# Start and end of a two-layer decoder trunk: whole first weight tiles, x cast in one piece, more idle products, another order of the last down products

## The chip, the core and the metric

The kernel runs on one core of a Trainium2 chip. The time is the device time of one execution in microseconds; lower is better. Only the matrix engine (TensorE, PE in the rows) multiplies; ScalarE (ACT) and VectorE (DVE) prepare its operands, GpSimd (POOL) does little, and SyncE (SP) issues the transfers from main memory.

## The reference

Two layers, each a half-step SwiGLU feed-forward block (FFN), a token mixer, and a second FFN. The sequence is 256 tokens of width 1024, the FFN is 2816 wide. All is float32.

```python
def swiglu(x, w_gate, w_up, w_down):
    return (jax.nn.silu(x @ w_gate) * (x @ w_up)) @ w_down

for l in range(DEPTH):
    x = layer_norm(ALPHA * x + 0.5 * swiglu(x, ffn1_gate[l], ffn1_up[l], ffn1_down[l]), ln_g[l, 0], ln_b[l, 0])
    ...
    x = layer_norm(ALPHA * x + mix, ln_g[l, 1], ln_b[l, 1])
    x = layer_norm(ALPHA * x + 0.5 * swiglu(x, ffn2_gate[l], ffn2_up[l], ffn2_down[l]), ln_g[l, 2], ln_b[l, 2])
```

## The kernel before

**Products in three parts.** Every float32 operand is split into a high half (a cast to the type fp32r, by ScalarE) and a low half (the operand minus the high half, by VectorE); `halves` does both (lines 102 and 103). `mm3` then makes one product out of three (lines 96 to 98), in this order: x high by weight high, x high by weight low, x low by weight high. The second one is therefore the first that needs the weight's low half.

**Weights.** They come in tiles of 128 x 1024 floats (512 KB) through five raw buffers: a transfer on SyncE (line 140), then `halves` into a ring of finished tiles. A tile of gate and up weights holds two of the eight steps of the width 1024, here kt 0 to 7: kt 0 and 1 in weight 0, kt 2 and 3 in weight 1, and so on; the left 512 columns belong to the even kt. The width of the FFN is cut into 11 groups (`NG`), of 256 gate and 256 up columns; the tokens into two halves (`hf`) of 128.

**The start.** The first group's four weights are not loaded as all the others are. `FFN.start` (the first FFN only) cuts each of them into two halves of 512 columns, and x, which lies transposed in memory, into pieces of 1, 1, 2, 2 and 2 kt (`cuts`). SyncE issues a piece of x and then the weight halves that go with it. The order of ScalarE and VectorE is written out by hand in a string: `X2` splits the third piece of x (for each token half apart), `W3` the half of a weight for kt 3, `M3` issues the six products of kt 3 (`pair`: three for either token half). TensorE's own order is by hand everywhere: the order of the code. While the first transfers are on their way, TensorE does `WARM` products of a tile of zeros (line 381).

**The rest.** Behind the start a scheduler orders ScalarE and VectorE, with priorities for the steps that TensorE waits for; the order of TensorE and the transfers' order stay that of the code.

**The end.** `D(g, hf)` multiplies group g's result by its two down weights: six products into the left accumulator (`c` = 0, columns 0 to 511), then six into the right one (`c` = 1). The last calls are D(8, 1), D(9, 1) and D(10, 1); behind the last one `layer_norm` (lines 252 to 262) adds the residual and takes statistics of either half on VectorE, and the result is stored. The operand of D(10, 1) is transposed by TensorE (line 409) and split by ScalarE and VectorE only while D(9, 1) runs: a counter of products (`later`) puts the transposes behind the fourth of the `mm3` calls that follow.

Of the kernel before, what the change touches and what calls it, by code (L numbers as in the profile page):

```python
# [10 lines left out]
F32 = mybir.dt.float32  # L11
# [3 lines left out]
ALU = mybir.AluOpType  # L15
PSUM = bass.MemoryType.PSUM

P = 128
D = 1024
# [5 lines left out]
NG = DFF // GW  # L25
# [13 lines left out]
AHEAD, BEHIND = 100, 400  # L39
PINNED, STARTED = 4, 4  # L40
HT = 6
WARM = 14


class Later:
# [29 lines left out]
def trunk(ctx: ExitStack, tc: tile.TileContext, t, out: bass.AP):  # L75
    nc = tc.nc
# [30 lines left out]
    class Weight:  # L107


        def __init__(self, src, ring, bufs, cuts=1):  # L110
            self.src, self.ring, self.bufs, self.cuts = src, ring, bufs, cuts
            self.uses = 2
            self.parts = None
            stream.append(self)

        def load(self):
            p = wp if self.ring == "w" else scope[0]
            older = rings.setdefault(self.ring, []) if p else None
            if p is None or len(older) >= self.bufs and older[-self.bufs].uses:
                return False  # L120
            older.append(self)
            self.raw = rawp.tile([P, ET], F32, name="raw")
            wh = p.tile([P, ET], F32R, name=self.ring + "h", bufs=self.bufs)
            wl = p.tile([P, ET], F32R, name=self.ring + "l", bufs=self.bufs)
            self.parts = (wh, wl)
            if self.cuts == 1:
                self.fetch(0)
                first, second = self.split(0)
                if position[0] < STARTED + 6:
                    tc.keep_in_program_order(first)  # L130
                if pinned[0]:
                    tc.keep_in_program_order(second)
                pinned[0] = max(0, pinned[0] - 1)
            return True
# [134 lines left out]
    class FFN:  # L269
        def __init__(self, l, w, ln_i, first=False, last=False):  # L270
            gu, dn = t["gu"][l, w], t["dn"][l, w]
            self.first, self.last, self.mixer_next = first, last, not w
            self.slots = ((16, 18), (16, 18) if w else (13, 14))
            self.accs = [None, None]
            self.gw, self.dw, self.ht = {}, {}, {}
            self.ln = (l, ln_i)
            self.gb = None
            for g in range(NG):
                self.gw[g] = []
                for kq in range(4):  # L280
                    extra = (4 * g + kq) % (NW + NX) >= NW
                    self.gw[g].append(Weight(gu[g, kq], *(("x", NX) if extra else ("w", NW)),
                                             2 if first and g == 0 else 1))
                for n in {0: [], 1: [0, 1], 2: [], NG - 1: [NG - 2, NG - 1]}.get(g, [g - 1]):
                    self.dw[n] = [Weight(dn[2 * n + i], "d", ND) for i in range(2)]

# [62 lines left out]
        def start(self):  # L349

            ws = self.gw[0]
            for w in ws:
                w.load()
            position[0] = STARTED
            pinned[0] = 6
            cuts = (0, 1, 2, 4, 6, 8)
            xr = [xp.tile([P, KT // 2, S], F32, name="x") for _ in range(2)]
            arrived = lambda a, b: xr[a // 4][:, a % 4:a % 4 + b - a, :]
            for a, b in zip(cuts, cuts[1:]):
                nc.sync.dma_start(arrived(a, b), t["xT"][:, a:b, :])  # L360
                for k in range(a, b):
                    ws[k // 2].fetch(k % 2)
            for hf in range(2):
                xT[hf] = Transposed(hf, None, cuts=cuts)
            ps = [psa.tile([P, 2 * GW], F32, name="acc") for _ in range(2)]

            def split_x(n):
                a, b = cuts[n], cuts[n + 1]
                for hf in range(2):
                    halves(xT[hf].h[:, a:b, :], xT[hf].l[:, a:b, :], arrived(a, b)[:, :, hf * P:(hf + 1) * P])  # L370
                    xT[hf].done = b

            def multiply(kt):
                self.pair(kt, ws, ps)


            zero = scope[0].tile([P, 256], mybir.dt.bfloat16, name="zero")
            nc.vector.memset(zero, 0.0)
            idle = psg.tile([P, 512], F32, name="gu")[:, 0:256]
            for _ in range(WARM):  # L380
                nc.tensor.matmul(idle, zero[:, 0:P], zero, start=True, stop=True)
            with tc.manual_schedule(engines={mybir.EngineType.Activation, mybir.EngineType.DVE}):
                for what in "X0 W0 M0 X1 W1 M1 X2 W2 M2 W3 M3 X3 W4 M4 W5 M5 X4 W6 M6 W7 M7".split():
                    {"X": split_x, "W": lambda k: ws[k // 2].split(k % 2), "M": multiply}[what[0]](int(what[1]))
            for w in ws:
                w.uses = 0
            advance()
            for hf in range(2):
                self.gate(0, hf, ps[hf])
            ps = [psg.tile([P, 2 * GW], F32, name="gu") for _ in range(2)]  # L390
            for kt in range(KT):
                self.pair(kt, self.gw[1], ps)
                if kt % 2:
                    self.gw[1][kt // 2].uses = 0
                    advance()
            for hf in range(2):
                self.gate(1, hf, ps[hf])
# [15 lines left out]
                halves(hth, htl, pt)  # L413
            self.ht[g, hf] = (hth, htl)

        def D(self, g, hf):
            if self.turned(g):
                ht = [[p[:, place[hf], :] for p in self.ht[g, i]] for i in range(2)]
            else:
                later.wait(lambda: (g, hf) in self.ht)  # L420
                ht = [[p[:, i, :] for p in self.ht[g, hf]] for i in range(2)]
            if g == 0:
                self.accs[hf] = [psa.tile([P, 512], F32, name="acc") for _ in range(2)]
            if g == 4 and hf == 0:
                self.gb = load_gb(*self.ln)
                if self.first:
                    load_consts()
                    for n in range(2):
                        load_x(n)
            dw = [w.parts for w in self.dw[g]]  # L430
            for c in range(2):
                cs = slice(c * 512, c * 512 + 512)
                for i in range(2):
                    mm3(self.accs[hf][c], ht[i][0], ht[i][1], dw[i][0][:, cs], dw[i][1][:, cs],
                        g == 0 and i == 0, g == NG - 1 and i == 1)
            for w in self.dw[g]:
                w.used()
            if g == NG - 1:
                layer_norm(hf, self.accs[hf], 0.5 / ALPHA, self.gb, self.slots[hf], self.last)

        def run(self):
# [29 lines left out]
            if self.first:  # L471
                with tc.high_priority(offset=-BEHIND):
                    lower_bounds()
            for g in range(NG - 3, NG):
                D(g, 1)


    def lower_bounds():
# [399 lines left out]
```

## Time and profile before

| | us |
|---|---|
| three runs | 966.07, 968.62, 968.62 |
| median | 968.62 |
| the profiled execution, its time | 968.72 |
| its span, first to last instruction | 967.0 |
| TensorE busy | 956.0 |
| VectorE busy | 653.5 |
| ScalarE busy | 520.0 |

The span and all rows are of one profiled execution. A time of the trace counts from the first instruction. In a row of the timeline the first number is the start, the second the length; a row that ends in x2 holds two instructions, and brackets give the engine's idle time ahead of it and what ended that. A product's length in these rows is longer than its step, since products overlap: how fast TensorE goes is read from the distance of two starts.

### The profile page before, as it was taken

The page shows a single profiled execution, that of the slowest core. Times are in us where ns is not written, and L with a number is a line of the kernel's source. Part 1 is how long each engine was busy: PE and PEld are TensorE (multiplying, and loading weights), DVE is VectorE, ACT ScalarE, POOL GpSimd, SP SyncE. Part 2 cuts the span into 40 slices and gives each one's busy share as a digit, 9 for nine tenths or more (in the row PEclk, how much of TensorE's full clock was granted, in tenths as well). Part 3 has the DMA queues.
Part 4 walks back from the last instruction along what each step waited for, and adds up shares of the span by engine and source line. Part 5 has one row for each costly group of instructions (what it writes and reads, how often), then busy time and mean ns, then how long its engine had stood idle before and what let it go on. Part 6 is the DMA issues. An engine that isn't in the chain of part 4 may idle for free. (4 is left out here: it accounts for less than half of the span.)

```text
span 967.0 us, 13131 instructions
## 1 busy us (share of the span) xinstructions
PE 956.0 (99%) x4814; PEld 806.9 (83%) x4814; DVE 653.5 (68%) x1093; ACT 520.0 (54%) x808; POOL 27.7 (3%) x50
## 2 busy tenths in 40 slices
PE   9999999999999999999999999999999999999996
PEld 7888888888887888888888888888888888888885
DVE  6875656669679775756676565647897896665625
ACT  6766554367455656454446555433965466645420
POOL 0000000010010000000000000000001000000000
PEclk9999999999999999999999999999999999999999
DMA  8977775333436867564346766543334377766301
GB/s 282 339 257 264 253 244 175 112 109 132 154 109 215 308 218 240 191 208 168 119 162 242 236 209 215 167 153 98 129 133 155 103 266 282 228 224 205 127 1 44
DMA packets 51521, 180.68 MB, mean 187 GB/s; under 512 B 6272, under 2 KB 6528, under 8 KB 51456
## 3 DMA queue, kind: packets, MB, share of 16 engines
q1 hardware_dynamic: 51264, 179.31, 55.2%
q8 instruction: 38, 0.62, 0.2%
q0 software_dynamic: 192, 0.53, 0.2%
q14 instruction: 27, 0.22, 0.1%
HBM read 178.76 MB, written 1.05 MB: 186 GB/s over the span
## 5 line engine op out<-in xcount | busy, mean ns | idle before, releaser
L102 ACT CAST wh<-raw 128x1024 fp32r<-128x1024 f32 (+1 forms) x204 | 210.1, 1034 | 110.2 <-DMA raw<-in_gu 40.7
L103 DVE TENSOR_TENSOR wl<-raw,wh 128x1024 fp32r<-128x1024 f32 (+1 forms) x204 | 241.4, 1198 | 24.8 <-ACT wh L102 12.7
L310 PE MATMUL gu<-xt,wh 128*128 128x512 f32 x768 | 180.6, 391 | 0.0
L103 DVE TENSOR_TENSOR dl<-raw,dh 128x1024 fp32r<-128x1024 f32 x88 | 106.9, 1223 | 100.2 <-ACT dh L102 99.9
L310 PEld LDWEIGHTS gu<-xt,wh 128*128 128x128 f32 x768 | 144.1, 188 | 31.5
L102 ACT CAST dh<-raw 128x1024 fp32r<-128x1024 f32 x88 | 92.0, 1050 | 108.3 <-DMA raw<-in_dn 104.0
L96 PE MATMUL acc<-dh,hth 128*128 128x512 f32 x352 | 139.9, 397 | 0.0
L98 PE MATMUL acc<-dh,htl 128*128 128x512 f32 x352 | 138.2, 393 | 0.0
L97 PE MATMUL acc<-dl,hth 128*128 128x512 f32 x352 | 137.5, 391 | 0.2 <-DVE dl L103 0.2
L96 PE MATMUL gu<-wh,xt 128*128 128x512 f32 x336 | 135.0, 402 | 0.0
L98 PE MATMUL gu<-wh,xt 128*128 128x512 f32 x336 | 131.6, 392 | 0.0
L97 PE MATMUL gu<-wl,xt 128*128 128x512 f32 x336 | 131.3, 391 | 0.0
L310 PE MATMUL gu<-xt,wl 128*128 128x256 f32 x768 | 99.6, 282 | 0.0
L310 PEld LDWEIGHTS gu<-xt,wl 128*128 128x128 f32 x768 | 96.8, 191 | 1.9
L333 DVE TENSOR_TENSOR sil<-gu,sil 128x256 f32<-128x256 f32 x64 | 27.0, 422 | 92.0 <-ACT sil L332 92.0
L98 PEld LDWEIGHTS acc<-dh,htl 128*128 128x128 f32 x352 | 66.0, 188 | 14.8
L97 PEld LDWEIGHTS acc<-dl,hth 128*128 128x128 f32 x352 | 66.2, 188 | 13.2 <-DVE dl L103 0.8
L96 PEld LDWEIGHTS acc<-dh,hth 128*128 128x128 f32 x352 | 66.2, 188 | 12.0
L98 PEld LDWEIGHTS gu<-wh,xt 128*128 128x128 f32 x336 | 63.1, 188 | 13.6
L97 PEld LDWEIGHTS gu<-wl,xt 128*128 128x128 f32 x336 | 63.2, 188 | 12.6
L96 PEld LDWEIGHTS gu<-wh,xt 128*128 128x128 f32 x336 | 63.1, 188 | 12.4
L310 PE MATMUL gu<-xt,xh 128*128 128x512 f32 x256 | 62.4, 396 | 0.0
(157 smaller groups left out, 1026.7 us busy)
## 6 DMA issues: line engine op xcount, KB each, us to landing
raw<-in_gu SPq DMA_DIRECT2D x172, 512.0 KB, 4.3
raw<-in_dn SPq DMA_DIRECT2D x88, 512.0 KB, 4.6
raw<-in_win SPq DMA_DIRECT2D x40, 512.0 KB, 4.4
raw<-in_wout SPq DMA_DIRECT2D x16, 512.0 KB, 4.3
lng<-in_ln_g SPq DMA_DIRECT2D x6, 512.0 KB, 4.5
lnb<-in_ln_b SPq DMA_DIRECT2D x6, 512.0 KB, 5.8
raw<-in_gu SPq DMA_DIRECT2D x8, 256.0 KB, 6.3
raw<-in_cumM SPq DMA_DIRECT2D x2, 512.0 KB, 5.1
```

Of the source, the lines that this page charges most:

```text
L96: nc.tensor.matmul(ps, lh, wh, start=start, stop=False)
L97: nc.tensor.matmul(ps, lh, wl, start=False, stop=False)
L98: nc.tensor.matmul(ps, ll, wh, start=False, stop=stop)
L102: first = nc.scalar.copy(dst_h, src)
L103: return first, nc.vector.tensor_tensor(dst_l, src, dst_h.bitcast(F32), ALU.subtract)
L310: nc.tensor.matmul(ps[i][part][:, 2 * S - w:], weight.parts[lo][:, c:c + P], x[:, 0:w], start=kt == 0 and not lo, stop=kt == KT - 1 and lo ...
L333: nc.vector.tensor_tensor(dst, p[:, 0:S], dst, ALU.add)
```

## The change

- The first group's weights: only weight 0 is still fetched and split in two halves. Weights 1, 2 and 3 are fetched by one transfer of 512 KB each and split by one cast of 1024 columns and one subtraction. The new parameter `by_hand` keeps all four out of the usual loading.
- Of each pair of transfers the weight's is now issued first, then the piece of x. Since there are as many pieces of x as fetches (five), the whole weight 1 now goes ahead of the x piece of kt 2 and 3, weight 2 ahead of that of kt 4 and 5.
- A piece of x is split for both token halves by one instruction; the first piece's cast is done by VectorE, not ScalarE.
- `WARM` is 17 instead of 14.
- In the last FFN the last three D of the second token half are taken by halves of columns, in the order (8, left), (9, left), (8, right), (10, left), (9, right), (10, right).

```diff
-WARM = 14
+WARM = 17
...
-            if self.cuts == 1:
+            if not self.by_hand:
                 self.fetch(0)
...
-                                             2 if first and g == 0 else 1))
+                                             2 if first and g + kq == 0 else 1, first and g == 0))
...
             for a, b in zip(cuts, cuts[1:]):
+                ws[a // 2].fetch(a % 2)
                 nc.sync.dma_start(arrived(a, b), t["xT"][:, a:b, :])
-                for k in range(a, b):
-                    ws[k // 2].fetch(k % 2)
...
                 a, b = cuts[n], cuts[n + 1]
+                h, l = (xt2[:, a:b, m].rearrange("p k h t -> p k (h t)") for m in range(2))
+
+                (nc.vector.tensor_copy if n == 0 else nc.scalar.copy)(h, arrived(a, b))
+                nc.vector.tensor_tensor(l, arrived(a, b), h.bitcast(F32), ALU.subtract)
                 for hf in range(2):
-                    halves(xT[hf].h[:, a:b, :], xT[hf].l[:, a:b, :], arrived(a, b)[:, :, hf * P:(hf + 1) * P])
                     xT[hf].done = b
...
-                for what in "X0 W0 M0 X1 W1 M1 X2 W2 M2 W3 M3 X3 W4 M4 W5 M5 X4 W6 M6 W7 M7".split():
+                for what in "X0 W0 M0 X1 W1 M1 X2 W2 M2 M3 X3 W4 M4 M5 X4 W6 M6 M7".split():
...
-        def D(self, g, hf):
+        def D(self, g, hf, cols=(0, 1)):
...
-            for c in range(2):
+            for c in cols:
...
+            if 1 not in cols:
+                return
...
-            for g in range(NG - 3, NG):
-                D(g, 1)
+            if self.last:
+
+                for g, c in ((NG - 3, 0), (NG - 2, 0), (NG - 3, 1), (NG - 1, 0), (NG - 2, 1), (NG - 1, 1)):
+                    D(g, 1, (c,))
+            else:
+                for g in range(NG - 3, NG):
+                    D(g, 1)
```

The order of SyncE's first transfers, before (raw is the buffer of a weight, in_gu the gate and up weights, x a piece of x):

```order
L360 DMA x<-in_xT 128x256
L140 DMA raw<-in_gu 128x512
L360 DMA x<-in_xT 128x256
L140 DMA raw<-in_gu 128x512
L360 DMA x<-in_xT 128x512
L140 DMA raw<-in_gu 128x512 x2
L360 DMA x<-in_xT 128x512
L140 DMA raw<-in_gu 128x512 x2
```

and now:

```order
L140 DMA raw<-in_gu 128x512
L361 DMA x<-in_xT 128x256
L140 DMA raw<-in_gu 128x512
L361 DMA x<-in_xT 128x256
L140 DMA raw<-in_gu 128x1024
L361 DMA x<-in_xT 128x512
L140 DMA raw<-in_gu 128x1024
L361 DMA x<-in_xT 128x512
```

The third piece of x (the first of 128x512) stood behind two half weights and two pieces; now two half weights, two pieces and the whole weight 1 stand ahead of it.

VectorE at the start, before (xt is the split x, wl the low half of a weight, zero the tile of zeros):

```order
L378 MEMSET zero 128x128
L103 TENSOR_TENSOR xt<-x,xt 128x128 x2
L103 TENSOR_TENSOR wl<-raw,wh 128x512
L103 TENSOR_TENSOR xt<-x,xt 128x128 x2
L103 TENSOR_TENSOR wl<-raw,wh 128x512
L103 TENSOR_TENSOR xt<-x,xt 128x2x128 x2
L103 TENSOR_TENSOR wl<-raw,wh 128x512 x2
```

and now:

```order
L380 MEMSET zero 128x128
L370 CAST xt<-x 128x256
L371 TENSOR_TENSOR xt<-x,xt 128x256
L103 TENSOR_TENSOR wl<-raw,wh 128x512
L371 TENSOR_TENSOR xt<-x,xt 128x256
L103 TENSOR_TENSOR wl<-raw,wh 128x512
L371 TENSOR_TENSOR xt<-x,xt 128x2x256
L103 TENSOR_TENSOR wl<-raw,wh 128x1024
```

The first piece's cast came to VectorE, and the low half for kt 2 is one of 1024 columns; ScalarE's list has the same pieces in the same turn, its cast of weight 1 being one of 128x1024.

TensorE before its last products, before (one row of each six; acc_7611 is the left accumulator, acc_7612 the right one; hth_8583, hth_8735 and hth_8906 are of groups 8, 9 and 10):

```order
L96 MATMUL acc_7611<-dh_8462,hth_8583 128x512
...
L96 MATMUL acc_7612<-dh_8462,hth_8583 128x512
...
L96 MATMUL acc_7611<-dh_8614,hth_8735 128x512
...
L96 MATMUL acc_7612<-dh_8614,hth_8735 128x512
...
L96 MATMUL acc_7611<-dh_8670,hth_8906 128x512
...
L96 MATMUL acc_7612<-dh_8670,hth_8906 128x512
```

and now (acc_7595 is the left one, acc_7596 the right one; hth_8567, hth_8719 and hth_8890 are of groups 8, 9 and 10):

```order
L96 MATMUL acc_7595<-dh_8446,hth_8567 128x512
...
L96 MATMUL acc_7595<-dh_8598,hth_8719 128x512
...
L96 MATMUL acc_7596<-dh_8446,hth_8567 128x512
...
L96 MATMUL acc_7595<-dh_8654,hth_8890 128x512
...
L96 MATMUL acc_7596<-dh_8598,hth_8719 128x512
...
L96 MATMUL acc_7596<-dh_8654,hth_8890 128x512
```

The left half of group 10 moved from the fifth place to the fourth; the transposes of line 409 stand behind the second six in both.

## Rows read from the trace of the kernel before

**Rows 1.** Page, part 1: each engine's busy time, share of span, instructions.

```profile
PE 956.0 (99%) x4814; PEld 806.9 (83%) x4814; DVE 653.5 (68%) x1093; ACT 520.0 (54%) x808; POOL 27.7 (3%) x50
```

**Rows 2.** TensorE's waits: line, for whom, us in total, times, longest.

```profile
PE acc L96 <- ACT wh L102: 0.9, 1, 0.9
PE gu L186 <- DVE x L260: 0.7, 1, 0.7
```

**Rows 3.** Timeline, TensorE, the first 19 us.

```profile
1.06 3.17 PE L381 MATMUL gu<-zero 128*128 128x256 bf16 x14 [1.06 <-DVE zero L378]
5.15 0.79 PE L96 MATMUL acc<-wh,xt 128*128 128x512 f32 x1 [0.92 <-ACT wh L102]
5.88 0.79 PE L97 MATMUL acc<-wl,xt 128*128 128x512 f32 x1
...
9.45 0.63 PE L96 MATMUL acc<-wh,xt 128*128 128x512 f32 x1
9.88 0.55 PE L97 MATMUL acc<-wl,xt 128*128 128x512 f32 x1
10.26 0.39 PE L98 MATMUL acc<-wh,xt 128*128 128x512 f32 x1
10.49 0.39 PE L96 MATMUL acc<-wh,xt 128*128 128x512 f32 x1
10.71 0.47 PE L97 MATMUL acc<-wl,xt 128*128 128x512 f32 x1
...
18.76 0.39 PE L96 MATMUL gu<-wh,xt 128*128 128x512 f32 x1
```

**Rows 4.** Timeline, ScalarE, the first 17 us.

```profile
4.48 0.62 ACT L102 CAST wh<-raw 128x512 fp32r<-128x512 f32 x1 [0.79 <-DMA raw<-in_gu]
...
8.38 0.71 ACT L102 CAST xt<-x 128x256 fp32r<-128x256 f32 x2 [1.87 <-DMA x<-in_xT]
9.29 1.28 ACT L102 CAST wh<-raw 128x512 fp32r<-128x512 f32 x2 [0.21 <-DMA raw<-in_gu]
...
15.29 1.05 ACT L102 CAST wh<-raw 128x1024 fp32r<-128x1024 f32 x1 [0.65 <-DMA raw<-in_gu]
```

**Rows 5.** Timeline, VectorE, the first 18 us.

```profile
9.94 1.36 DVE L103 TENSOR_TENSOR wl<-raw,wh 128x512 fp32r<-128x512 f32 x2 [0.36 <-ACT wh L102]
...
16.37 1.23 DVE L103 TENSOR_TENSOR wl<-raw,wh 128x1024 fp32r<-128x1024 f32 x1 [1.00 <-ACT wh L102]
```

**Rows 6.** Timeline, SyncE: issues of x's third piece and weight 1.

```profile
2.59 0.44 SPq L360 DMA_DIRECT2D x<-in_xT  x1
3.07 0.91 SPq L140 DMA_DIRECT2D raw<-in_gu  x2
```

**Rows 7.** Transfers issued at 2.7:3.0 and 3.6:3.9; last number, us from issue to landing.

```profile
x<-in_xT SPq DMA_DIRECT2D x1, 256.0 KB, 5.8
...
raw<-in_gu SPq DMA_DIRECT2D x1, 256.0 KB, 6.4
```

**Rows 8.** Stretches: length, busy time of each engine, granted clock, DMA share, GB/s.

```profile
3.00:6.00 3.00, 2.08 (x8) 0.97 (x6) 1.37 (x5) 1.62 (x6) 0.00 (x0) 1.00 0.82 253
6.00:9.00 3.00, 3.00 (x7) 2.35 (x8) 1.10 (x4) 1.13 (x3) 0.00 (x0) 1.00 0.92 246
9.00:12.00 3.00, 3.00 (x12) 2.28 (x11) 2.63 (x7) 2.59 (x6) 0.00 (x0) 1.00 1.04 397
```

**Rows 9.** Timeline of the end, TensorE and VectorE.

```profile
954.16 0.42 DVE L103 TENSOR_TENSOR htl<-gu,hth 128x256 fp32r<-128x256 f32 x1 [2.50 <-ACT hth L102]
...
954.95 0.39 PE L96 MATMUL acc<-dh,hth 128*128 128x512 f32 x1
...
957.87 0.69 DVE L252 SCALAR_TENSOR_TENSOR x<-acc,x 128x512 f32<-128x512 f32 x1 [3.28 <-PE acc L98]
...
958.80 0.39 PE L98 MATMUL acc<-dh,htl 128*128 128x512 f32 x1
...
959.23 0.69 DVE L252 SCALAR_TENSOR_TENSOR x<-acc,x 128x512 f32<-128x512 f32 x1
```

More of the change, by code (lines that the diff above doesn't have):

```diff
@@ L107, in trunk, with __init__ @@
     class Weight:
-        def __init__(self, src, ring, bufs, cuts=1):
-            self.src, self.ring, self.bufs, self.cuts = src, ring, bufs, cuts
+        def __init__(self, src, ring, bufs, cuts=1, by_hand=False):
+            self.src, self.ring, self.bufs, self.cuts, self.by_hand = src, ring, bufs, cuts, by_hand
             self.uses = 2
```

## The prediction

> **What bounds the kernel now.** I read the page's engine totals first: TensorE is busy 956.0 of 967.0 us [rows 1], so a gain or a loss exists only where TensorE stands still or runs slowly. The waits of TensorE behind the start are then few: 0.9 us for the first weight cast, 0.7 us for a layer norm in the middle, the others smaller [rows 2]. What the totals hide stands in TensorE's timeline of the first 19 us [rows 3]. The 14 idle products run from 1.06 to 4.23; the first real product comes at 5.15, the second at 5.88, because it needs the low half of the first weight. From there products are 0.43 us apart (9.45 to 9.88: 512 columns, that is 1.2 GHz), and only from about 10.2 on 0.23 us apart (10.26 to 10.49; 2.4 GHz). The granted-clock column says 1.00 for all of it [rows 8]; before 10.2 the spacing contradicts it, and I go by the spacing. After the 36 products of kt 2 to 7 the next group starts at 18.76: from the second product of kt 2 (10.71) that is 35 steps in 8.05 us, without a gap worth naming. So whatever moves that second product of kt 2 moves 18.76, and with a TensorE that is full to the end, the end.
>
> What sets 10.71 is data as much as the clock. ScalarE waited 1.87 us for the third piece of x and cast it at 8.38, then waited for the first half of weight 1 and cast the two halves from 9.29 in 1.28 us, 0.64 each [rows 4]. VectorE made the low halves from 9.94 in 1.36 us, 0.68 each [rows 5], so the first was there at 10.6. Product 10.71 waited for just that.
>
> **Part 1, the start: transfers.** SyncE issued the third x piece (kt 2 and 3, 256 KB) at 2.59, with 768 KB queued ahead of it; it took 5.8 us, so it lay at 8.4 with 1024 KB in. The second half of weight 1 was issued at about 3.5 and took 6.4 us: 1536 KB in by 9.9 [rows 6, 7]. The transfers moved 253 and 246 GB/s up to 9 us, and 397 from then on [rows 8]. The new order puts all of weight 1 (512 KB) ahead of that x piece, which now completes 256+128+256+128+512+256 = 1536 KB. By bytes it lands where 1536 KB landed: 9.9 instead of 8.4. Ten issues replace thirteen, at some 0.45 us each [rows 6], but an issue was not what x waited for.
>
> **Part 2, the start: casts.** For kt 2 the lists of ScalarE and VectorE now read: x piece, then the whole weight 1. ScalarE: x as one 128x512 cast, taken as a half weight (0.64 us), then the whole tile, 1.05 us [rows 4]; VectorE's low half of the whole tile takes 1.23 us [rows 5]. From 9.9: x high at 10.6, weight high at 11.65, weight low at 12.9 (0.05 us of hand-over in the sum). The x low half (about 0.7 us on VectorE) lies beside the weight cast. TensorE starts kt 2 at 11.7 and does its second product at 12.9 instead of 10.71: **+2.2 us**. It is good for 12 products at once, since both kt 2 and 3 are in the tile, and kt 4 follows at 12.9 + 11 x 0.23 = 15.4. Its data: the fourth x piece now completes 2304 KB; at 0.26 MB per 0.66 us (397 GB/s) that is three half tiles after 9.9, 11.9. From there 0.64 + 1.05 + 1.23 gives 14.9 once the engines are free. That cover is 0.5 us. For kt 6 the same sum is 17.0 against 18.1. So no second stall.
>
> The first products. Weight 0 now goes first, but with x the same 384 KB must be in: the second of the two lands near 4.5, as ScalarE's cast of the first half weight shows [rows 4]. VectorE then casts x, subtracts for its low half and only then makes the weight's low half: 0.42 + 0.42 + 0.68 after 4.5 is 6.0 (0.42 is a 128x256 subtraction [rows 9], taken for the cast too, which the trace does not show on VectorE). So the first product may come at 4.9 instead of 5.15, but the second at about 6.0 against 5.88. Cost of this part: between -0.3 and +0.3 us on kt 0, and nothing at the end, since kt 0 and 1 end at 6.0 + 11 x 0.43 = 10.7, before kt 2 has its data at 11.7. The three idle products (0.23 us each [rows 3], 0.7 in all) end at about 4.9: nothing by themselves.
>
> Here a rule is to be weighed. Idle products did not raise the clock in this trace: it rose after some 4.3 us of close products, from 5.88 to 10.2 [rows 3]. The Trainium skill, TensorE: Matmul & The Clock Gate, Part 1, says that the array starts at half rate and activity releases it, and that the moment varies from run to run; by it, denser idle products could give full rate from kt 0 on. By the trace, kt 0 and 1 would then end 2.0 us earlier (10 steps of 0.43 made 0.23), and wait 2.0 us longer for the same weight: the sum stays +2.2. What it raises is the chance of the first rival.
>
> **Part 3, what follows.** The scheduler swaps some casts of ScalarE and VectorE in the first layer's FFN; TensorE there has no wait in the trace [rows 2]. The next group's first weight had its low half at 17.6, its product was at 18.76 [rows 3, 5]; now it follows the last weight of group 0 on VectorE (17.0 + 1.23 = 18.2) against 20.9. Taken as 0; if that cover failed it would show as tenths, like the waits in [rows 2].
>
> **Part 4, the last down products.** The left 512 columns are finished 12 products before the end instead of 6, so VectorE can do their residual step and statistics 1.4 us sooner. Before, the first began at 957.87 and took 0.69, the second takes as long, and the right half's step began at 959.23, when the last product (958.80, 0.39 us) had just ended at 959.19 [rows 9]. So 0.05 us is to be had, no more. The new order needs the last transposed operand two half-steps earlier: where a product of the group before now starts at 954.95; its low half is ready at 954.58 [rows 9]. Cover 0.37 us. Taken: -0.05.
>
> **Sum.** +2.2 - 0.05 = +2.15. The profiled execution took 968.72 (span 967.0 and 1.72 around it), the median of the three runs is 968.62: they are the same case. 968.62 + 2.15 = **970.8**. The one run at 966.07 shows that a start can go 2.5 us better by itself. Bounds of the one large term: the x piece lands between 8.4 (unmoved, +0.7) and 10.5 (weight 1 passed wholly at the slow 250 GB/s, 2.1 us, +2.8). I take bytes, since rows with equal bytes in are at hand.
>
> **Rivals.**
> 1. *The clock falls or stays low in the new gap.* From 10.7 to 12.9 TensorE has one product to do. If the clock is at half rate behind that, it pays again what it paid here: about 10 steps at 0.43 instead of 0.23, 2.0 us. Time 970.8 + 2.0 = 972.8, **slower beyond 0.3%**. For it: before, after 0.92 us without work, products were slow for over 4 us. Against: the rest of the trace has no such gap after the rise, so none is seen to bring it down. It decides if kt 2 and 3 are 0.43 apart. The Trainium skill's same page (the table of its closing part on kernels) warns of idle gaps between bursts, which speaks against this change. Chance 0.20.
> 2. *Fewer, larger descriptors end the slow stretch early.* Weights now move 4 KB a row. Were 397 GB/s reached from 3 us on, the 1.5 MB that moved from 3 to 9 us [rows 8] would take 3.8 us instead of 6; 1536 KB are then in at 7.7 instead of 9.9, the second product of kt 2 has its data at 10.7, and TensorE arrives for it at 10.9: +0.2, or 0.0 with an early rise of the clock. Time 968.7, **not slower**. For it: the slow rate is of the stretch in which half rows and thirteen issues were in hand. Against: half tiles moved at 397 GB/s after 9 us, so the row length was not what slowed them. The Trainium skill, DMA: Bandwidth & Descriptors (Anatomy of one DMA), prices a transfer at 2.0 us and bytes by 436 GB/s; by it the x piece would be in at 6.4 and, with the clock up early, the time 1.3 us below before, 967.3. But by it the old x piece would have been in at 5.2, and the trace has 8.4: the measurement decides. Chance 0.20.
> 3. *A gain of over 0.3%*, 2.9 us: even with 0.23 us from the first product at 5.15 on, 47 steps end at 16.1 instead of 18.76, 2.7 us. Chance 0.02.
>
> **How the numbers follow.** The forecast holds 0.58. 0.3% of 968.62 is 2.9 us, about what a measurement of this kernel can tell from no change; the forecast itself lies inside it. Slower by more: rival 1 (0.18 of its 0.20) and the forecast's upper end (0.06). Faster by more: 0.03 with run-to-run luck. Within: 0.73. The range goes from 967.8 (rival 2 and some luck of the start) to 973.0 (most of rival 1).
>
> **What would show it.** Right: TensorE's first product near 4.9, the second near 6.0; a wait of about 1 us for a weight's high half at kt 2 and another of about 1 us for its low half, none at kt 4 and 6; ScalarE waiting for x until 9.9; the second group starting near 20.9. Wrong: x of kt 2 landing by 8, products 0.43 apart after 13, or waits in the FFN behind it. The end: the right half's residual step beginning within 0.1 us of the last product.

## The result and the profile after

| | before | after |
|---|---|---|
| median of 11 runs each, us | 967.05 | 970.77 |
| lowest and highest | 966.07 to 968.62 | 968.83 to 974.51 |
| ratio, 95% interval | | 1.0036, 1.0023 to 1.0048 |
| the profiled execution | 968.72 | 969.78 |
| its span | 967.0 | 968.0 |

The changed kernel is 3.7 us slower by the medians. The two profiled executions lie only 1.0 us apart, since before's is above all of its 11 runs and after's lies a microsecond under its median; so the traces show a mechanism, and the medians its price.

TensorE's busy time in after, page part 1 and its waits, to be read beside [rows 1, 2] (engine, line, for whom; us in total, times, longest):

```profile
PE 955.6 (99%) x4817; PEld 805.8 (83%) x4817; DVE 652.8 (67%) x1086; ACT 518.7 (54%) x799; POOL 28.4 (3%) x50
```

```profile
PE acc L96 <- ACT wh L102: 1.4, 2, 1.0
PE acc L97 <- DVE wl L103: 1.2, 3, 0.8
PE gu L383 <- DVE zero L380: 1.1, 1, 1.1
PE gu L411 <- DVE hn L344: 0.7, 1, 0.7
```

The first two rows are 2.6 us of waits for a weight's high and low half, in five places; before has one such wait, 0.9 us for a high half. They all lie in the first 12 us, as TensorE's timeline of after shows (compare [rows 3]):

```profile
1.06 3.81 PE L383 MATMUL gu<-zero 128*128 128x256 bf16 x17 [1.06 <-DVE zero L380]
4.60 0.77 PE L96 MATMUL acc<-wh,xt 128*128 128x512 f32 x1
5.57 0.50 PE L97 MATMUL acc<-wl,xt 128*128 128x512 f32 x1 [0.20 <-DVE wl L103]
5.90 0.39 PE L98 MATMUL acc<-wh,xt 128*128 128x512 f32 x1
6.13 0.40 PE L96 MATMUL acc<-wh,xt 128*128 128x512 f32 x1
...
8.03 0.50 PE L96 MATMUL acc<-wh,xt 128*128 128x512 f32 x1 [1.04 <-ACT wh L102]
...
10.56 0.51 PE L96 MATMUL acc<-wh,xt 128*128 128x512 f32 x1 [0.38 <-ACT wh L102]
11.82 0.50 PE L97 MATMUL acc<-wl,xt 128*128 128x512 f32 x1 [0.76 <-DVE wl L103]
12.16 0.39 PE L98 MATMUL acc<-wh,xt 128*128 128x512 f32 x1
...
19.91 0.39 PE L96 MATMUL gu<-wh,xt 128*128 128x512 f32 x1
```

Products are 0.23 us apart from 5.90 on (5.90 to 6.13), not from 10.2 on as before: full rate for kt 0 and 1. It gains nothing, since kt 2 still waits for its data. TensorE now stands still ahead of kt 1 (8.03), ahead of kt 2 (10.56) and between kt 2's first and second product (11.82). From there to 19.91 there is no gap, so the second group starts 1.15 us later than before (18.76).

ScalarE and VectorE of after, the rows that answer to [rows 4, 5]:

```profile
7.05 0.40 ACT L370 CAST xt<-x 128x256 fp32r<-128x256 f32 x1 [2.59 <-DMA x<-in_xT]
7.37 0.61 ACT L102 CAST wh<-raw 128x512 fp32r<-128x512 f32 x1
8.94 0.62 ACT L370 CAST xt<-x 128x512 fp32r<-128x512 f32 x1 [0.97 <-DMA x<-in_xT]
9.47 1.04 ACT L102 CAST wh<-raw 128x1024 fp32r<-128x1024 f32 x1
```

```profile
4.16 0.29 DVE L370 CAST xt<-x 128x256 fp32r<-128x256 f32 x1 [3.16 <-DMA x<-in_xT]
4.49 0.43 DVE L371 TENSOR_TENSOR xt<-x,xt 128x256 fp32r<-128x256 f32 x1
4.83 0.68 DVE L103 TENSOR_TENSOR wl<-raw,wh 128x512 fp32r<-128x512 f32 x1
...
10.54 1.23 DVE L103 TENSOR_TENSOR wl<-raw,wh 128x1024 fp32r<-128x1024 f32 x1 [0.26 <-ACT wh L102]
```

The chain into 11.82 reads from x's third piece: landed by 8.94, x cast, weight cast 9.47 to 10.51, low half 10.54 to 11.77. The piece for kt 1 landed only at 7.03 (4.79 before), which is the wait at 8.03. The stretches beside [rows 8] (length, busy time of each engine, granted clock, DMA share, GB/s):

```profile
3.00:6.00 3.00, 2.80 (x12) 1.69 (x11) 1.32 (x3) 0.62 (x1) 0.00 (x0) 1.00 0.87 200
6.00:9.00 3.00, 1.74 (x7) 0.90 (x6) 1.12 (x2) 0.98 (x3) 0.00 (x0) 1.00 1.00 376
9.00:12.00 3.00, 1.87 (x7) 0.98 (x7) 2.15 (x3) 2.59 (x4) 0.00 (x0) 1.00 1.03 407
```

The fast stretch of the transfers began at 6 us instead of 9, behind a slower one (200 against 253 GB/s).

The end, beside [rows 9]: the last transposed operand's low half, the last product, and the right half's residual step.

```profile
955.14 0.42 DVE L103 TENSOR_TENSOR htl<-gu,hth 128x256 fp32r<-128x256 f32 x1 [2.50 <-ACT hth L102]
...
957.48 0.69 DVE L252 SCALAR_TENSOR_TENSOR x<-acc,x 128x512 f32<-128x512 f32 x1 [1.92 <-PE acc L98]
...
959.77 0.39 PE L98 MATMUL acc<-dh,htl 128*128 128x512 f32 x1
960.20 0.69 DVE L252 SCALAR_TENSOR_TENSOR x<-acc,x 128x512 f32<-128x512 f32 x1 [1.30 <-PE acc L98]
```

The left half's step now starts 2.3 us ahead of the last product (0.9 before), and it changes nothing: from the last product to the end of the span it is 8.23 us, before 8.20.

### The profile page after: what moved, and what is told of

Same layout as the page of the kernel before. It is cut to its first block, busy times and chain, and to the rows that moved or that the text cites. A ratio compares the mean times of both kernels' runs of the same rounds, so it can differ in the third digit from the quotient of the medians.

```text
span 968.0 us, 13118 instructions
## 1 busy us (share of the span) xinstructions
PE 955.6 (99%) x4817; PEld 805.8 (83%) x4817; DVE 652.8 (67%) x1086; ACT 518.7 (54%) x799; POOL 28.4 (3%) x50
## 4 chain that ended last, share of the span: by engine, by line
PE 66%; DVE 2%; DMA 1%; ACT 0%; issue 0%; DVEq 0%; SPq 0%
PE gu L310 28%; PE acc L98 7%; PE acc L97 7%; PE acc L96 7%; PE gu L98 5%; PE gu L97 5%; PE gu L96 5%; DMA raw<-in_dn 1%; PE acc L669 1%; DVE wl L103 1%; PE gu L186 1%; PE gu L411 0%; PE acc L642 0%; PE acc L641 0%; DVE x L260 0%
```

## The experiments

The runs are of four sets, each beside runs of the kernel before. The last three sets were made on three different chips, so kernels of different sets are to be compared by their distance from the before beside them. "Second product" is that of kt 2, "second group" its first product, both in the profiled execution. The last column counts the runs whose mean granted clock is 0.996 or less; the others have 0.997 to 0.999.

| run | median | ratio to before, 95% | second product | second group | runs at 0.996 or less |
|---|---|---|---|---|---|
| after | 970.77 | 1.0023 to 1.0048 | 11.82 | 19.91 | 3 of 11 |
| after_again | 971.77 | 1.0028 to 1.0053 | 11.88 | 19.95 | 2 of 5 |
| tail_alone | 968.08 | 0.9993 to 1.0011 | 10.82 | 18.75 | 0 of 11 |
| warm_alone | 967.59 | 0.9992 to 1.0010 | 10.24 | 18.35 | 0 of 11 |
| start_alone | 969.34 | 1.0012 to 1.0030 | 12.12 | 20.18 | 1 of 11 |
| halves | 968.43 | 1.0002 to 1.0020 | 11.04 | 19.10 | 0 of 11 |
| split_casts | 968.97 | 1.0007 to 1.0025 | 11.40 | 19.48 | 0 of 11 |
| x_first | 971.35 | 1.0024 to 1.0051 | 12.48 | 22.17 | 4 of 5 |
| x_first_halves | 968.04 | 0.9996 to 1.0014 | 10.04 | 18.11 | 2 of 11 |
| fill | 970.74 | 1.0018 to 1.0041 | 12.41 | 20.46 | 0 of 6 |
| x_first_fill | 970.49 | 1.0020 to 1.0040 | 12.35 | 20.49 | 0 of 8 |
| fine_x | 967.04 | 0.9988 to 1.0006 | 9.69 | 17.74 | 0 of 11 |
| before_again | 967.17 | 0.9988 to 1.0006 | 10.10 | 18.17 | 0 of 11 |

Before beside them: 967.05 (with after), 967.67 (28 runs, with tail_alone, warm_alone, halves, fill), 967.80 (21, with after_again, start_alone, x_first, x_first_halves), 967.45 (30, with the rest). Of these last 79 runs of the kernel before, three are at 0.996 or less: two of the 28, one of the 21, none of the 30.

**The two small parts alone**, on the kernel before. tail_alone has the new order of the last D only:

```diff
...
-            for g in range(NG - 3, NG):
-                D(g, 1)
+            if self.last:
+                for g, c in ((NG - 3, 0), (NG - 2, 0), (NG - 3, 1), (NG - 1, 0), (NG - 2, 1), (NG - 1, 1)):
+                    D(g, 1, (c,))
...
```

> The kernel before with the new order of the last six down half-steps and nothing else. Theory (all of the loss is made at the start): within 0.1 us of before, the right half's residual step beginning within 0.05 us of the last product, as it does after the whole change. Rival (the new order costs at the end, by a late transposed operand): 0.3 us or more slower, with a wait of TensorE behind 953. Its start is that of before, so its trace also tells where kt 2 of before begins in a second execution; the medians of 11 runs differ by 3.7 us while the two profiled spans differ by 1.0, so before's profiled start should have been a slow one: second product of kt 2 at 9 to 10 us instead of 10.71.

Measured: 968.08 against 967.67, ratio 1.0002; nothing to be told from no change. In its trace the last product starts at 957.30 and the right half's step at 957.72, 0.03 after that product's end. The forecast for its start missed: the second product came at 10.82, not at 9 to 10.

warm_alone:

```diff
-WARM = 14
+WARM = 17
```

> The kernel before with 17 idle products instead of 14 and nothing else. Theory (kt 2 waits for its data, not for TensorE): between 0.6 us faster and 0.1 us slower than before, the clock rising by about 5 to 7 us instead of 10.2 and kt 0 and 1 done earlier, but the second product of kt 2 no earlier than the low half of its weight. Rival (the early rise of the clock is worth its 2 us): 1.5 us or more faster than before.

Measured: 967.59 against 967.67. Its TensorE timeline:

```profile
1.06 3.81 PE L381 MATMUL gu<-zero 128*128 128x256 bf16 x17 [1.06 <-DVE zero L378]
5.16 0.79 PE L96 MATMUL acc<-wh,xt 128*128 128x512 f32 x1 [0.29 <-ACT wh L102]
...
6.22 0.39 PE L98 MATMUL acc<-wh,xt 128*128 128x512 f32 x1
6.46 0.40 PE L96 MATMUL acc<-wh,xt 128*128 128x512 f32 x1
...
10.24 0.50 PE L97 MATMUL acc<-wl,xt 128*128 128x512 f32 x1 [0.23 <-DVE wl L103]
```

So the three idle products alone bring full rate at about 6 us: products are 0.24 apart at 6.22, where before has 0.43 until 10.2. In all four traces with 14 idle products full rate came between 8.4 and 10.5, in the ten with 17 between 4 and 7. But kt 2 still waits for its weight: at most 0.5 us is left of the 2 us that kt 0 and 1 gain, and it does not show in the median.

**Which part of the start.** start_alone is the change without the two small parts:

```diff
-WARM = 17
+WARM = 14
...
-            if self.last:
+            if False:
```

> The transfers and casts of the change alone: 14 idle products and the old order of the last down products. Theory (the loss is of this part): 2.5 to 3.5 us slower than before, like the whole change within 0.7 us. The clock rises late, as before, so kt 0 and 1 take 0.43 us a product and fill the waits; the second product of kt 2 comes at about 11.8 all the same. Rival (the earlier rise of the clock, followed by gaps, is what costs): within 1.5 us of before.

Measured: 969.34 against 967.80, +1.5 us, where 2.5 to 3.5 were expected and the rival had up to 1.5; its second group starts at 20.18, later than after's. So this part alone does not make the whole loss in the median. halves is the whole change, but with all four first weights fetched and split in halves of 512 columns; the weights still go ahead of x:

```diff
-                                             2 if first and g + kq == 0 else 1, first and g == 0))
+                                             2 if first and g == 0 else 1, first and g == 0))
...
-                ws[a // 2].fetch(a % 2)
+                for k in range(a, b):
+                    ws[k // 2].fetch(k % 2)
```

(and the string of steps as before). 

> The whole change, but all four first weights fetched and split in halves of 512 columns as before; the weight's transfers still go ahead of the piece of x. Theory (of the loss at kt 2, the whole tile's longer cast and subtraction make 0.41 + 0.55 = about 1 us, the x piece behind 512 KB the rest): 1 us faster than the whole change, 1 to 2.5 us slower than before. Rival (larger transfers are what the change gains by): as slow as the whole change or slower. If the spread of the whole change comes from the clock falling while TensorE waits at kt 1 and 2, it gets smaller here, since the gap does.

Measured: 968.43 against 967.67, +0.8 us; 1 to 2.5 were expected. x_first is the whole change with each piece of x issued ahead of its weight, the weights whole; x_first_halves is both:

```diff
             for a, b in zip(cuts, cuts[1:]):
-                ws[a // 2].fetch(a % 2)
                 nc.sync.dma_start(arrived(a, b), t["xT"][:, a:b, :])
+                ws[a // 2].fetch(a % 2)
```

> The whole change, but each piece of x issued ahead of its weight, as before; weights 1 to 3 still whole. Theory (order and size both cost at kt 2): the x piece lands 1 us earlier, at about 8; the whole weight 1 at 9 to 9.5, and its low half is there 1.05 + 1.23 later, at 11.3 to 11.8: 1 to 2.5 us slower than before and up to 1 us faster than the whole change. Rival (the order of issue is the whole loss): within 0.5 us of before.

> What is left of the change when x goes first and all four weights are halves: x split in one piece (its first cast on VectorE), 17 idle products, the new order at the end. Theory (only the order of issue and the whole tiles cost): between 0.7 us faster and 0.3 us slower than before, the second product of kt 2 at 10.0 to 10.7. Rival (the x casts in one piece, or the first one on VectorE, cost): 1 us slower or more, with a late low half at kt 0 or 1.

Measured: 971.35 and 968.04 against 967.80, +3.6 us (1 to 2.5 were expected) and +0.2 us (as expected). With after and halves they make a square, each against before beside it: whole tiles +3.7 and in after_again +4.0 (weights first) and +3.6 us (x first), halves +0.8 and +0.2. So halves are worth about 3 us in either order, and the order half a microsecond with halves. With whole tiles no gain of the order is to be seen, but four of x_first's five runs have a low clock (see below). x's third piece landed only 0.2 us sooner in x_first, where 1 us was expected (ScalarE's cast is at 8.79, in after at 8.94), and the whole weight 1 then came last:

```profile
8.79 0.62 ACT L370 CAST xt<-x 128x512 fp32r<-128x512 f32 x1 [2.18 <-DMA x<-in_xT]
10.12 1.04 ACT L102 CAST wh<-raw 128x1024 fp32r<-128x1024 f32 x1 [0.72 <-DMA raw<-in_gu]
```

kt 2 needs both, and the pair is complete when the last byte of the two is in. Halves need 256 KB less for that. To tell the transfer's size from the cast's, split_casts fetches weights 1 to 3 whole, but casts and subtracts them in halves:

```diff
+        def whole(self):
+            nc.sync.dma_start(self.raw, self.src)
...
-                ws[a // 2].fetch(a % 2)
+                ws[0].fetch(a) if a < 2 else ws[a // 2].whole()
```

> The changed kernel with weights 1, 2 and 3 fetched whole as there, but cast and subtracted in halves of 512 columns. Theory (most of the loss at the start is the longer cast and subtraction of a whole tile, the rest is x landing later): x's third piece lands near 8.9 as in the changed kernel, the half's cast ends 0.4 us sooner, the half's subtraction takes 0.7 instead of 1.23, the second product of kt 2 comes at 10.9 to 11.0 instead of 11.82, the next group at 19.0 instead of 19.91, and the median is 969.0 to 970.0, about 1 to 1.5 us under the changed kernel's 970.8. Rival (what costs is the transfer by whole tiles, since the other transfers then land later): the second product of kt 2 within 0.3 us of 11.8 and the time as the changed kernel's. If the waits of tenths near 328 us come from whole tiles being loaded, they stay here; if they come from the altered order of the casts, they go.

Measured: 968.97 against 967.45, +1.5 us, so 2.2 of after's 3.7 us are gone with the longer instructions (what the clock has in them follows below). ScalarE and VectorE there:

```profile
9.40 0.62 ACT L373 CAST xt<-x 128x512 fp32r<-128x512 f32 x1 [1.04 <-DMA x<-in_xT]
9.92 1.14 ACT L102 CAST wh<-raw 128x512 fp32r<-128x512 f32 x2
```

```profile
10.05 0.69 DVE L374 TENSOR_TENSOR xt<-x,xt 128x512 fp32r<-128x512 f32 x1 [0.96 <-ACT xt L373]
10.66 1.29 DVE L103 TENSOR_TENSOR wl<-raw,wh 128x512 fp32r<-128x512 f32 x2
```

The second product came at 11.40, not at 10.9 to 11.0 as expected: x landed at 9.4 in this run instead of 8.9. From x's landing to that product it is 2.0 us, in after 2.9; the 0.9 us that the shorter instructions were to give are there. They would have given more, but VectorE's low half of x (10.05, 0.69) now ends last ahead of the weight's low half at 10.66, which the long weight cast had hidden.

**The clock.** The whole change is 3.7 and 4.0 us above the before beside it (970.77, 971.77), start_alone 1.5, though the other two parts cost nothing alone. The runs' clocks point to it: of after's 16 runs (both sets) the 11 at 0.997 or more have a median of 969.96, the five below 972.42. Such a clock is not of these kernels alone: 3 of before's 79 runs and 2 of x_first_halves' 11 have it too. x_first's profiled execution has such a clock, and its TensorE timeline shows where:

```profile
8.59 0.39 PE L98 MATMUL acc<-wh,xt 128*128 128x512 f32 x1
11.22 0.50 PE L96 MATMUL acc<-wh,xt 128*128 128x512 f32 x1 [2.24 <-ACT wh L102]
12.48 0.50 PE L97 MATMUL acc<-wl,xt 128*128 128x512 f32 x1 [0.76 <-DVE wl L103]
...
13.51 0.51 PE L98 MATMUL acc<-wh,xt 128*128 128x512 f32 x1
13.82 0.63 PE L96 MATMUL acc<-wh,xt 128*128 128x512 f32 x1
14.24 0.63 PE L97 MATMUL acc<-wl,xt 128*128 128x512 f32 x1
...
17.16 0.39 PE L98 MATMUL acc<-wh,xt 128*128 128x512 f32 x1
17.39 0.39 PE L96 MATMUL acc<-wh,xt 128*128 128x512 f32 x1
...
22.17 0.39 PE L96 MATMUL gu<-wh,xt 128*128 128x512 f32 x1
```

and its stretches with the granted clock (the number before the last two):

```profile
12.00:15.00 3.00, 2.52 (x8) 2.04 (x9) 2.85 (x4) 2.55 (x3) 0.00 (x0) 0.77 1.03 414
15.00:18.00 3.00, 3.00 (x10) 2.35 (x10) 2.85 (x3) 2.40 (x4) 0.00 (x0) 0.66 0.92 314
```

TensorE had full rate, stood still for 2.24 us, did one product, stood still for another 0.76; then, with all its data there, its products were 0.42 apart from 13.82 to 16.80 and 0.23 again from 17.16. Two runs put idle products into the gaps: fill into after's (6 each ahead of kt 1, ahead of kt 2 and behind kt 2's first product), x_first_fill into x_first's:

```diff
...
             def multiply(kt):
-                self.pair(kt, ws, ps)
+                if kt == 2:
+                    fill(16)
+                self.pair(kt, ws, ps, fill if kt == 2 else None)
...
```

(`fill(n)` issues n products of zeros; `pair` calls it with 5 behind the first product.) fill has `fill(6)` for kt 1 and 2, and 6 in `pair`.

> The whole change with idle products put into the gaps of the start: 6 ahead of kt 1, 6 ahead of kt 2, 6 between the first and the second product of kt 2 (0.11 us each at full rate). Their results are not used. Theory that the spread of the whole change (968.83 to 974.51, mean granted clock 0.998 in the fast ones, 0.995 in the slow ones) is the clock falling in those gaps: mean clock 0.998 in all runs, times within 1.5 us of each other, median 969 to 970. Rival (the spread is that of the transfers, as in the sum): the same spread and median as the whole change, or up to 0.5 us more.

> x_first (the whole change with each piece of x issued ahead of its weight) with 16 idle products ahead of kt 2 and 5 more between its first and second product; nothing of the computation is left out. Theory (in part of the runs the clock falls to half because TensorE stands still for 2.2 and then 0.8 us there): the idle products fill both gaps, the mean granted clock is 0.997 or more in every run, no stretch from 12 to 19 us has a clock below 1.00, the next group starts at 20.0 to 20.5 where x_first's profile had 22.2, and the median is 969 to 970, that is 1.5 to 2.5 us under x_first's 971.35. Rival (the clock is let down by something else, by chance or by the load of the memory): the same share of runs at 0.996 or less, median within 0.5 us of 971.35. Second rival (the idle products stand in the way of the real ones): clock always up, but no gain, with products of kt 2 starting behind an idle one.

Measured: no clock below 0.997 in 14 runs, where after and x_first had 9 in 21. But these 14 runs are of two other chips than x_first's, and on one of those no run of any kernel has a low clock (71 runs, the 8 of x_first_fill among them). So the count alone does not show that the idle products did it. x_first_fill's TensorE:

```profile
8.30 1.92 PE L386 MATMUL gu<-zero 128*128 128x256 bf16 x16
11.09 0.49 PE L411 MATMUL acc<-wh,xt 128*128 128x512 f32 x1 [0.87 <-ACT wh L102]
11.43 0.72 PE L386 MATMUL gu<-zero 128*128 128x256 bf16 x5
12.35 0.50 PE L413 MATMUL acc<-wl,xt 128*128 128x512 f32 x1 [0.20 <-DVE wl L103]
...
20.49 0.39 PE L96 MATMUL gu<-wh,xt 128*128 128x512 f32 x1
```

The same data came at the same time (12.35 against 12.48), the products behind stayed 0.23 apart, and the second group started at 20.49 instead of 22.17. That is the fall's price, 1.55 us with the 0.13 taken off. These two traces, one of either kernel, bear the theory on the clock out; that filled gaps keep the clock up in every run is not shown. The forecast of the median missed: 970.49 is 0.9 us under x_first's and, beside the before of either set, +3.0 against +3.6 us; 1.5 to 2.5 us were expected. And fill, with no low clock in its six runs, has after's median (+3.1 us beside its own before; 969 to 970 was expected). In its trace the second product came at 12.41, 0.6 later than after's, because x's third piece landed 0.6 later (9.51 against 8.92). Filling a gap does not give back the time that the gap costs.

**Repeats.** after_again is the changed kernel, before_again the kernel before, for second traces.

> The whole change once more, beside its parts on one chip. In its first profile the second group began at 19.91, 1.15 us later than in before's, but 11 timed runs of it were 3.5 us slower in the median. Theory (the start is paid in full, and before's profiled execution had lost about 1.4 us elsewhere, in waits of the layer norms, that most of its runs do not lose): median 969 to 971, second group at 19.5 to 21. Rival (something behind the start costs 1 to 2 us more): second group by 19.9 and 1.5 us or more of waits in the stretch between it and the last product, in this profile too.

> The kernel before, unchanged, for a second trace of it and for a look at how far two series of one kernel differ. Theory (the profiled execution of before was one of its slower ones, since it lost 1.4 us ahead of the products at 308 to 310 us by chance): ratio 1.000 within 0.001, a span of 965.0 to 966.0 instead of 967.0, the second group near 18.5 to 18.8, no wait of tenths near 328 us. Rival (967.0 is its usual span): 966.7 or more again.

Measured: the changed kernel's start came out alike (second group at 19.95 and 19.91). Its median of 971.77 lies above the 969 to 971 expected, and its trace is 2.0 us longer than after's behind the start, much as the rival had it. The kernel before took 965.9 of span instead of 967.0; its second group started at 18.17, since full rate came at 8.4, not 10.2, and the low half of kt 2's weight was begun at 9.35, not 9.94; and it did not lose the 0.7 us at a layer norm of [rows 2]. So the trace that the prediction was made from is on the high side for this kernel. The wait of tenths near 328 us that after_again's trace has (0.27 at 327.81), and which I had put on the whole tiles or on the altered order of the casts, is in before_again too, and not in after or x_first_fill, which have both:

```profile
325.24 0.44 PE L409 MATMUL gu<-ident,hn 128*128 128x128 f32 x2 [0.16 <-DVE hn L344]
```

That theory fell: such waits come and go between executions of one kernel.

**A better version?** fine_x is x_first_halves with the piece for kt 2 and 3 cut in two:

```diff
-            cuts = (0, 1, 2, 4, 6, 8)
+            cuts = (0, 1, 2, 3, 4, 6, 8)
...
```

> x_first_halves (x ahead of its weights, all four weights in halves, casts of x for both token halves, 17 idle products, new order of the end) with x's third piece cut in two pieces of one kt, each split by itself. Theory (the start is set by when x's piece for kt 2 lands, since 256 KB of 512 KB-and-more are queued there): the piece for kt 2 is 128 KB less late, 0.3 us at 400 GB/s and 0.5 us at 250, its cast 0.2 us shorter, so the second product of kt 2 comes at 9.4 to 9.7 instead of 10.04 and the median is 967.4 to 968.0, 0 to 0.6 us under x_first_halves (968.04) and not measurably faster than before. Rival (one more issue of 0.45 us on SyncE and one more fixed cost of a cast delay the weight halves behind it): second product of kt 2 at 10.0 or later, kt 3 waits, and no gain or 0.3 us of loss.

Measured: 967.04 against 967.45, ratio 0.9997 (0.9988 to 1.0006). Its second product is at 9.69, as expected, its second group at 17.74, the earliest of all; the median is under the 967.4 to 968.0 expected. It beats the changed kernel by over 3 us; against the kernel before the interval holds 1.

## Why the prediction was right, and where not

**The number.** 970.8 was forecast and 970.77 measured, but that is luck: two errors of 1.6 us cancel. The base was 968.62, the median of three runs of which two were high; over 11 runs it is 967.05. And the change cost 3.7 us, not 2.15. The step of the text that failed first is "they are the same case": the profile's time and the median agreed because both were high. Of the 3.7 us, about 1 goes with the three runs of a low clock (the other eight have a median of 969.76), 1.15 to 1.74 with the later second group, by before's first and its second trace, and the rest stays open (parts 3 and 4 below).

**Part 1, the x piece.** This is the term that was mis-sized. By bytes it was to land at 9.9, 1.5 later than before; it landed at 8.9, 0.6 later. Equal bytes do not land at equal times in this stretch: it moved 376 GB/s from 6 to 9 us where before moved 246. The slow stretch did end early, as rival 2 had it, but not by its mechanism, larger transfers: the stretch moved 333 to 381 GB/s in the six traces with the weights first, halves among them, and 240 to 304 in the eight with x first, x_first with its whole tiles among them.

halves:

```profile
6.00:9.00 3.00, 1.70 (x6) 0.86 (x6) 1.12 (x2) 0.92 (x2) 0.00 (x0) 1.00 0.98 344
```

x_first:

```profile
6.00:9.00 3.00, 2.98 (x11) 2.07 (x10) 0.69 (x1) 0.82 (x2) 0.00 (x0) 1.00 0.92 292
```

So it goes with the order of issue; why, no run shows. Ahead of it the transfers moved 200 GB/s instead of 253, and the piece for kt 1 landed at 7.03 instead of 4.79. What the sum by bytes left out is the last part of a transfer. The trace has each landing in 16 parts, and the reader waits for the last. Of x's third piece in before, 11 parts had landed by 6.54, the last at 8.35, and its cast began at 8.38; of the half of weight 1 that gave the 9.9, 8 parts had landed by 7.80, the last at 9.93. In after, the parts of x's third piece came between 7.66 and 8.92. So the middle of that piece did move by 2.2 us (6.36 to 8.60), its end only by 0.6. In x_first its middle stayed at 6.22, and its last part came at 8.76. What holds the last parts back stays open.

By the prediction's estimate from the Trainium skill, DMA: Bandwidth & Descriptors (Anatomy of one DMA), x was to be in at 6.4; the trace has 8.9, and the measurement decides. That section prices transfers issued by GpSimd, and SyncE issued these, so the estimate was taken from another path than the one used here.

**Part 2, the casts.** The second product was to come 2.2 us later than before's; it came 1.1 us later than in before's first trace (10.71) and 1.7 later than in its second (10.10), since x landed sooner. From x's landing to it 3.0 us were forecast and 2.9 measured (8.94 to 11.82), with 1.04 for the cast of 1024 columns and 1.23 for its subtraction, as taken from rows of before. split_casts shows that it is these that cost: 0.9 us at that product. kt 4 and kt 6 did not wait, as said. Of the first products, 4.60 and 5.57 were measured where 4.9 and 6.0 were forecast: the pair landed 0.35 sooner than 4.5, and VectorE casts 128x256 in 0.29 us, not 0.42. The wait at kt 1 (1.04 us) was not foreseen; the text said that kt 0 and 1 end before kt 2 has its data, and so they do, so it costs nothing at the end of the chain. It is, though, one of the gaps in which TensorE stands still.

**The weighed rule.** The Trainium skill, TensorE: Matmul & The Clock Gate, Part 1, says that activity releases the clock. The traces of after and warm_alone agree (0.23 and 0.24 between products at 6 us): "idle products did not raise the clock in this trace" was true of 14 of them, not of 17. As the text worked out, full rate from kt 0 on gave nothing, since the wait for the weight took it back.

**Rival 1, the clock.** It was given 0.20, and it is real, for a part of the runs: x_first shows it with its stretch, 9 of 21 runs of after and x_first have a low mean clock, none of the 14 with the gaps filled (which were on other chips). The text's reason for it was a misreading, though: before had no full rate yet that could fall ahead of 10.2, since its 14 idle products took 0.23 us each, where x_first_fill's 16 in the gap took 0.12. Its price was put at 2.0 us; 1.55 was measured in the traces, 2.5 between after's runs (972.42 and 969.96). The text asked only whether it happens, not how often; a rival that strikes some executions moves the median by less than its price. The Trainium skill's same page (the table of its closing part on kernels) warns of idle gaps between bursts; the fall here followed gaps of 2.24 and 0.76 us, each shorter than those it warns of, so the trace goes beyond the page. The fall would also explain why 17 idle products, worth nothing alone, cost something beside whole tiles, which no run here tests by itself: in start_alone kt 0 and 1 run at half rate up to 10 us and fill the time in which after stands still, and one run in 11 has a low clock. That after's own falls come at the same place as x_first's, no trace shows; neither of its two profiled runs had one.

**Parts 3 and 4.** The end was forecast at -0.05 and is within 0.05; the transposed operand was in time, and no wait appeared. The scheduler's swaps were put at 0, and that held: from the second group's first product on, the traces of before and after run alike for 286 us (to 305.03 in before, 306.20 in after), and of all fourteen traces only split_casts differs there, by 0.5 us; the others agree within 0.06. Something else stays open: the 11 runs of after with an undisturbed clock have a median of 969.96, 2.2 to 2.9 us above before's 967.80 and 967.05, and the later second group explains 1.15 (by before's first trace) to 1.74 us (by its second). The rest, about 1 us, would have to lie behind the start: between second group and last product the two traces of after have 939.86 and 941.83 us, the two of before 940.04 and 939.62. All of these differences arise in three stretches, each with a layer norm in it (305 to 349, 484 to 544 and 761 to 824 us in before). They take 166.2 to 169.1 us together in the seven traces with whole first tiles, 165.8 to 167.3 in the seven with halves. The two ranges overlap, so one can't tell a cause from chance there, and I name none.

## What to carry to other kernels

At a start that waits for data, count to the last byte and the last instruction that the next product needs: a larger tile saves issues, but the first product waits for the last part of it, and its cast and its subtraction are longer by all that it does not need yet. Freeing one engine early, or raising its clock, gains nothing while the data come later, and it makes the gaps longer behind which the clock fell in one trace here; idle products in such a gap went with a clock that stayed up, but they do not give the gap back. And before a profile's time is taken as the base, see where it lies among more than three runs: here the base was off by as much as the change was mis-sized.

## What the runs showed of the hardware

- Three idle products go with when full rate comes: with 14 (ended at 4.23) between 8.4 and 10.5 us in four traces, with 17 between 4 and 7 us in ten.
- After full rate had been reached, stillness of 2.24 and 0.76 us was followed by half rate (products 0.42 apart from 13.8 to 16.8), not at once but five products later (x_first's trace). By the runs' mean clocks it strikes only a part of the executions; a low mean clock is also seen, more rarely, where there are no such gaps (3 of before's 79 runs).
- From 3 to 6 us the transfers move 253 GB/s in before and 200 in after, from 6 to 9 us 246 and 376, from 9 to 12 us 397 and 407. The fast second stretch goes with the order of issue, not with the size of the tiles: 333 to 381 in six traces with the weights first, 240 to 304 in eight with x first.
- The last of a transfer's 16 parts trails the middle one by 0.1 to 2.5 us at this start (x's third piece: 2.0 in before, 0.3 in after, 2.5 in x_first), and the reader waits for it.
- VectorE casts 128x256 from float32 to fp32r in 0.29 us; ScalarE takes 0.40 for the same, 0.62 for 128x512 and 1.04 for 128x1024.
